# A segment mean over 10 million sorted ids: probe groups spread between data tiles as small row groups, and the masked sums' index ramp kept in PSUM

## The chip, the cores and the metric

The kernel runs on one core of one Trainium2 chip. The metric is the device time of one execution, in microseconds (us); lower is better. Times are quoted as medians of the fast runs of one kernel. Executions of one kernel agree within about 1% (230.13 to 231.72 us before), and a single core has a slower state now and then; slow runs are not compared with fast ones. The engines are called as the profile calls them: DVE is VectorE, ACT is ScalarE, POOL is GpSimd, SP is SyncE, PE is TensorE.

## The reference

```python
n, num_segments = 10_000_000, 10000
data        = np.random.randn(n).astype(np.float32)
segment_ids = np.sort(np.random.randint(0, num_segments, n))      # int64, sorted

def reference(data, segment_ids):
    num_segments = int(segment_ids.max()) + 1
    sums, counts = np.zeros(num_segments, np.float32), np.zeros(num_segments, np.float32)
    np.add.at(sums, segment_ids, data)
    np.add.at(counts, segment_ids, 1)
    return sums / np.maximum(counts, 1)
```

The 40 MB of data must be read. Of the 80 MB of ids only samples are read, because the ids are sorted and a segment is about 1,000 elements long.

## The kernel before

Each of the 128 partitions holds 78,125 consecutive elements, cut into 98 rows of 800. At most one segment border is expected in a row (a check sends any other input down a slow general path, which never runs here). For each row the kernel does this:

1. A *probe load* (SP) reads every 160th id, five 8-byte elements to a row, for a group of rows at once.
2. The *first look* (DVE, small instructions) finds from the probes which 160 elements hold the border, and writes the position into `IDX`.
3. A *gather* (POOL, one for each row, 128 positions) fetches the 159 ids there from HBM into a slot of `GT`.
4. The *reduce* (DVE, six rows at a time) sums those ids; from the sum and `QQ` comes the border's exact place `KK`.
5. The *masked sum* (DVE) adds the elements left of the border, `iota < KK`. ACT adds up the whole row.
6. At the end, counts, carries and two tables put together the means.

```python
GROUPS = [6, 8, 12, 12, 12, 12, 12, 12, 12]      # rows of one probe load
RING = 36                                        # rows that GT can hold
...
iota = cpool.tile([P, L], FP32, name="iota")     # SBUF
GT = gpool.tile([P, RING, W], I64, name="GT")
nc.gpsimd.memset(GT.bitcast(I32).rearrange("p a b -> p (a b)"), 0)

def load_probes(g):
    a = 0 if g == 0 else K * bounds[g] + 1
    b = min(K * bounds[g + 1] + 1, NPR)
    nc.sync.dma_start(out=pr_flat[:, a:b], in_=ids_p[:, a * S : (b - 1) * S + 1 : S])

def first_look(g):
    ...                                           # copy, compare, reduce, scale, subtract
    nc.vector.tensor_add(out=pos, in0=ST[:, a:b], in1=wb[:, a:b])
    nc.vector.scalar_tensor_tensor(out=IDX[:, a:b], in0=NB[:, a:b], scalar=BIG, in1=pos, ...)

def gather(g):
    for r in range(bounds[g], bounds[g + 1]):
        nc.gpsimd.indirect_dma_start(out=GT[:, r % RING, :], in_=ids2d[:],
            in_offset=bass.IndirectOffsetOnAxis(ap=IDX[:, r : r + 1], axis=0), ...)

def second_look(a, b):                            # six rows
    nc.vector.tensor_reduce(out=GS[:, a:b], in_=gt32[:, s : s + b - a, 0 : 2 * W : 2], ...)
    kr = fpool.tile([P, b - a], FP32, name="kr")
    nc.vector.tensor_sub(out=kr, in0=QQ[:, a:b], in1=GS[:, a:b])
    nc.vector.tensor_mul(out=KK[:, a:b], in0=kr, in1=BT[:, a:b])

def split(r):                                     # the masked sum
    nc.vector.scalar_tensor_tensor(out=junk_v[:, 0:n], in0=iota[:, 0:n], scalar=KK[:, r : r + 1],
        in1=d, op0=ALU.is_lt, op1=ALU.mult, accum_out=A[:, r : r + 1])
...
load_probes(0); load_data(0); load_probes(1); load_data(1); load_probes(2)     # (shortened)
for r in range(-6, NR):
    while nt < NT and nt <= (r + 24) // 2:
        load_data(nt)                             # one data tile is two rows
        nt += 1
        if pnext < NG:
            load_probes(pnext)                    # so all nine stand before tile 9
            pnext += 1
    ...                                           # first looks 30 rows ahead, gathers 16 rows ahead
    if r >= done_k: second_look(done_k, min(done_k + 6, NR)); ...
    total(r)
    split(r)
    if r == IF_AT - 4: keys(); check()
    if r == IF_AT: counts(0, 60); with tc.If(...): general_path(...)
    ...
```

The order in which DVE gets its instructions is fixed when the program is built, and it is not the order of this source: in the trace the reduces, first looks and the small work of the check are mixed differently. DVE then works strictly in that order, as far as the traces show: in the changed kernel it stands still for 8.1 us before the reduce at 126.14 us, while five masked sums behind it have their data and their border places.

Of the kernel before, what the change touches and what calls it, by code (L numbers as in the profile page):

```python
# [8 lines left out]
FP32 = mybir.dt.float32  # L9
BF16 = mybir.dt.bfloat16  # L10
I32 = mybir.dt.int32
# [5 lines left out]
P = 128  # L17
D = 78125
L = 800
S = 160  # L20
K = L // S
NR = 98
# [2 lines left out]
E = 8  # L25
NX = NR + E
BIG = float(1 << 24)
GROUPS = [6, 8, 12, 12, 12, 12, 12, 12, 12]
RING = 36
N1 = 72  # L30
N2 = 8
# [146 lines left out]
def kernel(  # L178
# [6 lines left out]
    nc = tc.nc  # L185
    N = data.shape[0]
    NSEG = out.shape[0]
    assert N == P * D and NSEG == 10000 and sum(GROUPS) == NR

# [5 lines left out]
    cpool = ctx.enter_context(tc.tile_pool(name="cpool", bufs=1))  # L195
# [3 lines left out]
    ppool = ctx.enter_context(tc.tile_pool(name="ppool", bufs=1, space=bass.MemoryType.PSUM))  # L199
# [9 lines left out]
    snt = cpool.tile([P, 1], I64, name="snt")  # L209
# [3 lines left out]
    bounds = [0]  # L213
    for g in GROUPS:
        bounds.append(bounds[-1] + g)
# [5 lines that stand above are left out]
# [3 lines left out]
    def load_data(t):  # L224
        d = dpool.tile([P, 2 * L], FP32, name="data_t")
        a, b = 2 * t * L, min(2 * (t + 1) * L, D)
        nc.sync.dma_start(out=d[:, 0 : b - a], in_=data_p[:, a:b])
        tiles[t] = d


    i_i = cpool.tile([P, L], I32, name="i_i")
    iota = cpool.tile([P, L], FP32, name="iota")
    nc.gpsimd.iota(i_i, pattern=[[1, L]], base=0, channel_multiplier=0)
    nc.vector.tensor_copy(out=iota, in_=i_i)
    wb_i = cpool.tile([P, NR], I32, name="wb_i")
    wb = cpool.tile([P, NR], FP32, name="wb")
    nc.gpsimd.iota(wb_i, pattern=[[L, NR]], base=-W, channel_multiplier=D)
# [14 lines left out]
        out=plast, in0=pc, scalar1=float(P - 1), scalar2=1.0e6, op0=ALU.is_equal, op1=ALU.mult  # L252
# [25 lines left out]
    T = cpool.tile([P, NR], FP32, name="T")  # L278
    NB = cpool.tile([P, NX], FP32, name="NB")
    GT = gpool.tile([P, RING, W], I64, name="GT")  # L280
    nc.gpsimd.memset(GT.bitcast(I32).rearrange("p a b -> p (a b)"), 0)  # L281
    gt32 = GT.bitcast(I32)
    junk_v = cpool.tile([P, L], BF16, name="junk_v")
    junk_a = cpool.tile([P, L], BF16, name="junk_a")
# [1 line left out]
    def first_look(g):  # L286
        a, b = bounds[g], bounds[g + 1]
        n = b - a
        if b == NR:
            nc.vector.tensor_copy(out=vend, in_=snt32[:, 0:1])  # L290
            nc.vector.tensor_copy(out=pr32[:, NR - 1, 2 * (K - 1) : 2 * K], in_=snt32)
            nc.vector.tensor_copy(out=V[:, NR : NR + 1], in_=snt32[:, 0:1])
            nc.vector.tensor_copy(out=V[:, a:b], in_=pr32[:, a:b, 0])
        else:
            nc.vector.tensor_copy(out=V[:, a : b + 1], in_=pr32[:, a : b + 1, 0])  # L295
        eq = fpool.tile([P, n, K - 1], FP32, name="eq")
        in1b, in0b = bass.broadcast_tensor_aps(pr32[:, a:b, 0:1], pr32[:, a:b, 2 : 2 * K : 2])
        nc.vector.tensor_tensor(out=eq, in0=in0b, in1=in1b, op=ALU.is_equal)  # L298
        jc = fpool.tile([P, n], FP32, name="jc")
        nc.vector.tensor_reduce(out=jc, in_=eq, axis=AX.X, op=ALU.add)  # L300
        nc.vector.tensor_scalar(  # L301
            out=ST[:, a:b], in0=jc, scalar1=float(S), scalar2=float(1 + W), op0=ALU.mult, op1=ALU.add
        )
        if b == NR:
            nc.vector.tensor_scalar(
                out=ST[:, NR - 1 : NR], in0=ST[:, NR - 1 : NR], scalar1=float(LAST), scalar2=None,
                op0=ALU.min,
            )
        nc.vector.tensor_sub(out=BT[:, a:b], in0=V[:, a + 1 : b + 1], in1=V[:, a:b])  # L309
        nc.vector.tensor_scalar(  # L310
            out=NB[:, a:b], in0=BT[:, a:b], scalar1=-1.0, scalar2=1.0, op0=ALU.mult, op1=ALU.add
        )
        pos = fpool.tile([P, n], FP32, name="pos")
        nc.vector.tensor_add(out=pos, in0=ST[:, a:b], in1=wb[:, a:b])  # L314
        nc.vector.scalar_tensor_tensor(  # L315
            out=IDX[:, a:b], in0=NB[:, a:b], scalar=BIG, in1=pos, op0=ALU.mult, op1=ALU.add
        )
        nc.vector.scalar_tensor_tensor(  # L318
            out=QQ[:, a:b], in0=V[:, a:b], scalar=float(W), in1=ST[:, a:b], op0=ALU.mult, op1=ALU.add
        )  # L320

    def gather(g):
        for r in range(bounds[g], bounds[g + 1]):
            nc.gpsimd.indirect_dma_start(  # L324
                out=GT[:, r % RING, :],
                out_offset=None,
                in_=ids2d[:],
                in_offset=bass.IndirectOffsetOnAxis(ap=IDX[:, r : r + 1], axis=0),
                bounds_check=N - W,
                oob_is_err=False,  # L330
            )

    def second_look(a, b):
        s = a % RING
        nc.vector.tensor_reduce(  # L335
            out=GS[:, a:b], in_=gt32[:, s : s + b - a, 0 : 2 * W : 2], axis=AX.X, op=ALU.add
# [4 lines that stand above are left out]
# [139 lines left out]
    def counts(a, b):  # L480

        n = b - a
        ps = fpool.tile([P, n], FP32, name="ps")
        bp = fpool.tile([P, n], FP32, name="bp")
        ct = fpool.tile([P, n], FP32, name="ct")
        nc.vector.tensor_add(out=ps, in0=rp[:, a:b], in1=KK[:, a:b])
        nc.vector.tensor_mul(out=bp, in0=ps, in1=BT[:, a:b])
        nc.vector.tensor_tensor_scan(
            out=PS[:, a + 1 : b + 1], data0=NB[:, a:b], data1=bp, initial=PS[:, a : a + 1],
            op0=ALU.mult, op1=ALU.add,  # L490
        )
        nc.vector.tensor_sub(out=ct, in0=ps, in1=PS[:, a:b])
        nc.vector.tensor_scalar(out=ct, in0=ct, scalar1=1.0, scalar2=None, op0=ALU.max)
        nc.vector.reciprocal(out=ct, in_=ct)
        nc.vector.scalar_tensor_tensor(
            out=RB[:, PAD + a : PAD + b], in0=ct, scalar=nflag[:, 0:1], in1=BT[:, a:b],
            op0=ALU.mult, op1=ALU.mult,
        )

    def sums(a, b):  # L500

        c = min(b, NR)
        if c > a:
            nc.vector.tensor_sub(out=B[:, a:c], in0=T[:, a:c], in1=A[:, a:c])
# [50 lines left out]
    def write(o, i):  # L555
# [7 lines left out]

    NG = len(GROUPS)
    NT = (NR + 1) // 2
    load_probes(0)
    nc.vector.memset(snt32[:, 0:1], NSEG)
    nc.vector.memset(snt32[:, 1:2], 0)
    nc.sync.dma_start(
        out=snt[0 : P - 1, :],  # L570
        in_=segment_ids[D : N].rearrange("(p d) -> p d", d=D)[:, 0:1],
    )
    load_data(0)
    load_probes(1)
    load_data(1)
    load_probes(2)
    nt = 2

    IF_AT = 64
    C1 = 66  # L580
    C2 = 95
    done_k = 0
    gnext = 0
    lnext = 0
    pnext = 3
    for r in range(-6, NR):
        while nt < NT and nt <= (r + 24) // 2:
            load_data(nt)
            nt += 1
            if pnext < NG:  # L590
                load_probes(pnext)
                pnext += 1
        while lnext < NG and bounds[lnext] <= r + 30:
            first_look(lnext)
            lnext += 1
        while gnext < NG and bounds[gnext] <= r + 16:
            gather(gnext)
            gnext += 1
        if r < 0:
            continue  # L600
        if r >= done_k:
            b = min(done_k + 6, NR)
            second_look(done_k, b)
            done_k = b
        total(r)
        split(r)
        if r == E - 1:
            sums(0, E)
            carry(0, E)
            extend()  # L610
        if r == IF_AT - 4:
            keys()
            check()
        if r == IF_AT:
            counts(0, 60)
            with tc.If(nc.values_load(badi[0:1, 0:1], min_val=0, max_val=1) > 0):
                general_path(
                    tc, fpool, ppool, data, segment_ids, ids2d, odram, rdram, kdram, ident[:, 0:P], fbt
                )
        if r == C1 - 1:  # L620
            counts(60, C1)
            sums(E, C1)
            carry(E, C1)
            select1(0, 12)
            table1(0, 12)
        if done_k == NR and r == 96:
            counts(C1, NX)
            select1(12, N1 // 4)
            select2()
            sums(C1, C2)  # L630
            carry(C1, C2)
            table1(12, N1 // 4)
            write(out1, 0)
# [34 lines left out]
```

## Time and profile before

| | before |
|---|---|
| time, median of 4 fast runs | 231.38 us (230.13 to 231.72) |
| span of the profiled run | 230.0 us |
| DVE busy | 150.9 us (66%) |
| POOL busy | 128.9 us (56%), of it gathers 115.0 |
| first masked sum on DVE | 62.3 us |
| DVE waits for probe loads / for gathers | 40.5 us / 21.5 us |
| last instruction of DVE that counts as busy ends | 217.4 us |

These are the slices of the kernel before: the span in 40 equal parts of 5.75 us, each digit the busy share in tenths. The GB/s line has one number for each slice.

```profile
DVE  4963102204298960351999999999299999999800
POOL 8914777777778777777878788788400000000110
DMA  6899999999999999999999999999749000000000
GB/s 81 102 142 144 231 160 204 239 131 230 237 124 375 409 397 397 398 403 402 399 400 402 399 403 401 401 399 412 303 170 369 14 0 0 0 0 0 2 5 0
```

Until slice 12 (69 us) the DMA engines are busy and move only 81 to 240 GB/s, while the probe loads read single elements of 8 bytes (65,274 of the 74,701 packets of the run are under 512 bytes). Then they move 400 GB/s until the data ends (from 75 to 170 us 1,531 of 7,909 packets are under 512 bytes). DVE is nearly idle at first and full from slice 19 on. From its first gather at 19.7 us POOL is busy in one unbroken row until 164 us.

The costliest groups of the same profile: line, engine, operation, output and inputs, count; then busy time in us and the mean in ns; then the idle time of the engine just before and what ended most of it (`issue`: the engine waited for nothing that the profile shows).

```profile
L324 POOL DMA_INDIRECT GT<-in_segment_ids_dram,IDX x98 | 115.0, 1174 | 36.8 <-issue 26.2
L350 DVE SCALAR_TENSOR_TENSOR junk_v<-iota,q_114,data_t 128x800 bf16<-128x800 f32 x98 | 101.8, 1038 | 0.6
L295 DVE CAST q_114<-pr 128x13 f32<-128x13 int32 (+2 forms) x8 | 9.0, 1127 | 40.5 <-DMA pr<-in_segment_ids_dram 40.5
L335 DVE TENSOR_REDUCE GS<-GT 128x6 f32<-128x954 int32 (+1 forms) x17 | 18.7, 1099 | 23.1 <-DMA GT<-in_segment_ids_dram,IDX 21.5
L281 POOL MEMSET GT<- 128x11448 int32 x1 | 9.6, 9628 | 0.0
```

A gather takes 1.17 us on average and 0.3 us pass between two; apart from those 0.3 us, POOL waits only 10.6 us in all (36.8 - 26.2), most of it before the first gather. DVE's idle time stands in two places: 40.5 us at probe loads and 21.5 us at reduces that wait for gathered ids.

Five single instructions of the timeline (start, duration, instruction, idle time before it):

```profile
2.79 9.63 POOL L281 MEMSET GT<- 128x11448 int32 x1
4.83 7.62 DVE L295 CAST q_114<-pr 128x7 f32<-128x7 int32 x1 [2.39 <-DMA pr<-in_segment_ids_dram]
4.91 7.54 DVE L298 TENSOR_TENSOR eq<-pr 128x24 f32<-128x24 int32 x1
19.69 1.20 POOL L324 DMA_INDIRECT GT<-in_segment_ids_dram,IDX  x1 [7.27 <-DVE IDX L315]
62.31 1.04 DVE L350 SCALAR_TENSOR_TENSOR junk_v<-iota,q_114,data_t 128x800 bf16<-128x800 f32 x1
```

A cast of seven elements takes 7.62 us: it ends with the POOL memset, at 12.4 us. The first masked sum comes at 62.3 us, although its gathers had landed before 40 us.

### The profile page before, as it was taken

How to read it: one execution, taken by the hardware profiler on the slowest of the kernel's cores; microseconds unless marked ns; L12 is line 12 of the kernel's file. 1: busy time of each engine (PE TensorE's matmuls, PEld its weight loads, DVE VectorE, ACT ScalarE, POOL GpSimd, SP SyncE). 2: the span in 40 equal slices, each digit the busy share in tenths (PEclk: the TensorE clock that was granted, in tenths of full speed). 3: DMA queues.
4: the chain of work that ended last, by engine and by line, in shares of the span. 5: the costliest groups of instructions: out<-in, count | busy, mean ns of one | idle time of the engine just before them, and what ended most of it. 6: DMA issues, size and time to landing. Idle time of an engine off the chain costs nothing. (4 is left out here: it accounts for less than half of the span.)

```text
span 230.0 us, 1186 instructions
## 1 busy us (share of the span) xinstructions
PE 1.6 (1%) x6; PEld 1.4 (1%) x6; DVE 150.9 (66%) x432; ACT 95.4 (41%) x197; POOL 128.9 (56%) x114
## 2 busy tenths in 40 slices
PE   0000000000000100000000010000000000000000
PEld 0000000000000100000000000000000000000000
DVE  4963102204298960351999999999299999999800
ACT  2333023033032767676777787667746600000000
POOL 8914777777778777777878788788400000000110
DMA  6899999999999999999999999999749000000000
GB/s 81 102 142 144 231 160 204 239 131 230 237 124 375 409 397 397 398 403 402 399 400 402 399 403 401 401 399 412 303 170 369 14 0 0 0 0 0 2 5 0
DMA packets 74701, 53.39 MB, mean 232 GB/s; under 512 B 65274, under 2 KB 65357, under 8 KB 74688
## 3 DMA queue, kind: packets, MB, share of 16 engines
q1 hardware_dynamic: 69920, 40.51, 62.1%
q0 software_dynamic: 4768, 12.78, 19.2%
q14 instruction: 13, 0.11, 0.2%
HBM read 56.46 MB, written 0.04 MB: 246 GB/s over the span
## 5 line engine op out<-in xcount | busy, mean ns | idle before, releaser
L324 POOL DMA_INDIRECT GT<-in_segment_ids_dram,IDX x98 | 115.0, 1174 | 36.8 <-issue 26.2
L345 ACT ACTIVATE junk_a<-data_t 128x800 bf16<-128x800 f32 x98 | 85.0, 867 | 85.7 <-DMA data_t<-in_data_dram 81.7
L350 DVE SCALAR_TENSOR_TENSOR junk_v<-iota,q_114,data_t 128x800 bf16<-128x800 f32 x98 | 101.8, 1038 | 0.6
L295 DVE CAST q_114<-pr 128x13 f32<-128x13 int32 (+2 forms) x8 | 9.0, 1127 | 40.5 <-DMA pr<-in_segment_ids_dram 40.5
L335 DVE TENSOR_REDUCE GS<-GT 128x6 f32<-128x954 int32 (+1 forms) x17 | 18.7, 1099 | 23.1 <-DMA GT<-in_segment_ids_dram,IDX 21.5
L556 POOL DMA_INDIRECT out_dram<-out_139,AN x1 | 1.1, 1117 | 52.5 <-DVE FF L511 52.5
L345 ACT ACTIVATION_READ_ACCUMULATOR junk_a<-data_t 128x1 f32 x98 | 18.3, 186 | 0.0
L281 POOL MEMSET GT<- 128x11448 int32 x1 | 9.6, 9628 | 0.0
L298 DVE TENSOR_TENSOR eq<-pr 128x48 f32<-128x48 int32 (+2 forms) x9 | 9.2, 1025 | 0.0
L350 DVE DVE_READ_ACCUMULATOR junk_v<-iota,q_114,data_t 128x1 f32 x98 | 7.9, 81 | 0.0
L340 DVE TENSOR_TENSOR q_114<-kr,q_114 128x6 f32<-128x6 f32 (+1 forms) x17 | 2.7, 161 | 0.0
L339 DVE TENSOR_TENSOR kr<-QQ,GS 128x6 f32<-128x6 f32 (+1 forms) x17 | 2.7, 157 | 0.0
L301 DVE TENSOR_SCALAR ST<-jc 128x12 f32<-128x12 f32 (+2 forms) x9 | 2.1, 239 | 0.0
L556 POOL DMA_INDIRECT out_dram<-out_140,AN x1 | 1.0, 992 | 2.0 <-issue 2.0
L310 DVE TENSOR_SCALAR NB<-q_114 128x12 f32<-128x12 f32 (+2 forms) x9 | 1.8, 200 | 0.0
L300 DVE TENSOR_REDUCE jc<-eq 128x12 f32<-128x48 f32 (+2 forms) x9 | 1.7, 194 | 0.0
L345 ACT ACT_TABLE_LOAD x1 | 1.3, 1283 | 0.8 <-PEq L652 0.8
L314 DVE TENSOR_TENSOR pos<-ST,wb 128x12 f32<-128x12 f32 (+2 forms) x9 | 1.5, 164 | 0.1
L309 DVE TENSOR_TENSOR q_114<-q_114 128x12 f32<-128x12 f32 (+2 forms) x9 | 1.5, 166 | 0.1
L318 DVE SCALAR_TENSOR_TENSOR QQ<-q_114,ST 128x12 f32<-128x12 f32 (+2 forms) x9 | 1.5, 164 | 0.1
L315 DVE SCALAR_TENSOR_TENSOR IDX<-NB,pos 128x12 int32<-128x12 f32 (+2 forms) x9 | 1.5, 164 | 0.0
L527 DVE TENSOR_REDUCE out_139<-sel_133 128x48 f32<-128x624 f32 (+1 forms) x2 | 1.3, 628 | 0.0
(95 smaller groups left out, 29.5 us busy)
## 6 DMA issues: line engine op xcount, KB each, us to landing
data_t<-in_data_dram SPq DMA_DIRECT2D x48, 800.0 KB, 11.7
GT<-in_segment_ids_dram,IDX POOLq DMA_INDIRECT x98, 6.1
data_t<-in_data_dram SPq DMA_DIRECT2D x1, 662.5 KB
pr<-in_segment_ids_dram SPq DMA_DIRECT2D x6, 60.0 KB, 11.2
pr<-in_segment_ids_dram SPq DMA_DIRECT2D x1, 58.0 KB, 11.0
pr<-in_segment_ids_dram SPq DMA_DIRECT2D x1, 40.0 KB
pr<-in_segment_ids_dram SPq DMA_DIRECT2D x1, 31.0 KB, 4.0
snt<-in_segment_ids_dram SPq DMA_DIRECT2D x1, 1.0 KB
```

What stands on the lines that cost most here:

```text
L281: nc.gpsimd.memset(GT.bitcast(I32).rearrange("p a b -> p (a b)"), 0)
L295: nc.vector.tensor_copy(out=V[:, a : b + 1], in_=pr32[:, a : b + 1, 0])
L298: nc.vector.tensor_tensor(out=eq, in0=in0b, in1=in1b, op=ALU.is_equal)
L301: nc.vector.tensor_scalar(out=ST[:, a:b], in0=jc, scalar1=float(S), scalar2=float(1 + W), op0=ALU.mult, op1=ALU.add)
L310: nc.vector.tensor_scalar(out=NB[:, a:b], in0=BT[:, a:b], scalar1=-1.0, scalar2=1.0, op0=ALU.mult, op1=ALU.add)
L324: nc.gpsimd.indirect_dma_start(out=GT[:, r % RING, :], out_offset=None, in_=ids2d[:], in_offset=bass.IndirectOffsetOnAxis(ap=IDX[:, r : r ...
L335: nc.vector.tensor_reduce(out=GS[:, a:b], in_=gt32[:, s : s + b - a, 0 : 2 * W : 2], axis=AX.X, op=ALU.add)
L339: nc.vector.tensor_sub(out=kr, in0=QQ[:, a:b], in1=GS[:, a:b])
L340: nc.vector.tensor_mul(out=KK[:, a:b], in0=kr, in1=BT[:, a:b])
L345: nc.scalar.activation(out=junk_a[:, 0:n], in_=d, func=ACT.Copy, accum_out=T[:, r : r + 1])
L350: nc.vector.scalar_tensor_tensor(out=junk_v[:, 0:n], in0=iota[:, 0:n], scalar=KK[:, r : r + 1], in1=d, op0=ALU.is_lt, op1=ALU.mult, accum_ ...
L556: nc.gpsimd.indirect_dma_start(out=out2d[:], out_offset=bass.IndirectOffsetOnAxis(ap=AN[:, i : i + 1], axis=0), in_=o[:], in_offset=None,)
```

## The change

The change has five parts.

1. Eleven smaller probe groups, of 4, 6, 8 and then 10 rows, instead of nine of up to 12.
2. A probe load stands just before the data tile of its first row, instead of all of them before tile 9, so that the data comes in from the start.
3. The first look and its gathers stand 18 rows ahead of the masked sum (30 and 16 before).
4. `iota` lies in PSUM. The masked sum then reads one of its two large operands from PSUM. In the kernel before, the gathers from 21 to 62 us took 1.00 us each, and from the first masked sum on up to 1.83 us; that they would stay at 1.00 us with the ramp out of SBUF was the estimate from these figures.
5. The memset of `GT` is gone, and the check and the branch come at rows 78 and 82 instead of 60 and 64.

```diff
-GROUPS = [6, 8, 12, 12, 12, 12, 12, 12, 12]
+GROUPS = [4, 6, 8, 10, 10, 10, 10, 10, 10, 10, 10]
+X_PROBE = 26
+X_LOOK = 18
...
-    iota = cpool.tile([P, L], FP32, name="iota")
+    iota = ppool.tile([P, 1024], FP32, name="iota")
...
-    nc.gpsimd.memset(GT.bitcast(I32).rearrange("p a b -> p (a b)"), 0)
...
-    for r in range(-6, NR):
-        while nt < NT and nt <= (r + 24) // 2:
+    for r in range(-X_PROBE, NR):
+        while pnext < NG and bounds[pnext] <= r + X_PROBE:
+            load_probes(pnext)
+            pnext += 1
+            ...
+        while nt < NT and 2 * nt <= r + X_PROBE:
             load_data(nt)
             nt += 1
-            if pnext < NG:
-                load_probes(pnext)
-                pnext += 1
-        while lnext < NG and bounds[lnext] <= r + 30:
+        while lnext < NG and bounds[lnext] <= r + X_LOOK:
             first_look(lnext)
+            gather(lnext)
             lnext += 1
-        while gnext < NG and bounds[gnext] <= r + 16:
-            gather(gnext)
-            gnext += 1
...
-        if r == IF_AT - 4:
+        if r == CHECK_AT:                  # 78; IF_AT goes from 64 to 82
             keys()
             check()
...                                         # counts(0, 60), counts(60, C1) become counts(0, C1) after the branch
```

More of the change, by code (lines that the diff above doesn't have):

```diff
@@ L231 @@
     i_i = cpool.tile([P, L], I32, name="i_i")
-    iota = cpool.tile([P, L], FP32, name="iota")
+    iota = ppool.tile([P, 1024], FP32, name="iota")
     nc.gpsimd.iota(i_i, pattern=[[1, L]], base=0, channel_multiplier=0)
-    nc.vector.tensor_copy(out=iota, in_=i_i)
+    nc.vector.tensor_copy(out=iota[:, 0:L], in_=i_i)
     wb_i = cpool.tile([P, NR], I32, name="wb_i")
@@ L565 @@
     NT = (NR + 1) // 2
-    load_probes(0)
     nc.vector.memset(snt32[:, 0:1], NSEG)
     nc.vector.memset(snt32[:, 1:2], 0)
-    nc.sync.dma_start(
-        out=snt[0 : P - 1, :],
-        in_=segment_ids[D : N].rearrange("(p d) -> p d", d=D)[:, 0:1],
-    )
-    load_data(0)
-    load_probes(1)
-    load_data(1)
-    load_probes(2)
-    nt = 2
-    IF_AT = 64
+    CHECK_AT = 78
+    IF_AT = 82
     C1 = 66
@@ L584 @@
     lnext = 0
-    pnext = 3
-    for r in range(-6, NR):
-        while nt < NT and nt <= (r + 24) // 2:
+    pnext = 0
+    nt = 0
+    for r in range(-X_PROBE, NR):
+        while pnext < NG and bounds[pnext] <= r + X_PROBE:
+            load_probes(pnext)
+            pnext += 1
+            if pnext == 2:
+                nc.sync.dma_start(
+                    out=snt[0 : P - 1, :],
+                    in_=segment_ids[D : N].rearrange("(p d) -> p d", d=D)[:, 0:1],
+                )
+        while nt < NT and 2 * nt <= r + X_PROBE:
             load_data(nt)
             nt += 1
-            if pnext < NG:
-                load_probes(pnext)
-                pnext += 1
-        while lnext < NG and bounds[lnext] <= r + 30:
+        while lnext < NG and bounds[lnext] <= r + X_LOOK:
             first_look(lnext)
+            gather(lnext)
             lnext += 1
-        while gnext < NG and bounds[gnext] <= r + 16:
-            gather(gnext)
-            gnext += 1
         if r < 0:
@@ L610 @@
             extend()
-        if r == IF_AT - 4:
+        if r == CHECK_AT:
+            assert lnext == NG
             keys()
@@ L614 @@
         if r == IF_AT:
-            counts(0, 60)
+            assert nt == NT
             with tc.If(nc.values_load(badi[0:1, 0:1], min_val=0, max_val=1) > 0):
@@ L619 @@
                 )
-        if r == C1 - 1:
-            counts(60, C1)
+            counts(0, C1)
             sums(E, C1)
```

## The prediction

> **What bounds the kernel now.** Two phases.
>
> To 70 us the DMA engines do. The slices show them 90% busy, moving only 81 to 240 GB/s: probe loads read single 8-byte elements. In the timeline a 12-row probe load plus a data tile lands every 7.0 us before gathers start, every 9 us beside them; a data tile alone takes 2.0 to 2.6 us. I read: probe load 4.8 us, data tile 2.03, gathered row 0.31, additive. All nine probe loads stand before tile 9, and VectorE (DVE) takes first looks in order, so each waits for its load (40.5 us in the waits view). The first masked sum (L350) starts at 62.3 us.
>
> From 62 us DVE does: 98 masked sums 1.10 us apart, 17 reduces of gathered ids of 1.1 us. It also stands 23 us between 81 and 110 us, at reduces that wait for gathers. Data has ended by 182 us, DVE is full until 217.4: a backlog of 35 us. The span ends 12.6 us later.
>
> **What changes.**
> - Removed: the 9.63 us GpSimd memset of GT. Two DVE instructions take 7.6 us beside it. The first gather comes at 19.7 us, now about 7. Little alone: probes bound this phase.
> - Moved: 11 probe loads between data tiles. DMA work stays: 49 x 2.03 + 98 x 0.31 + 39 for probes + 2 start = 171 us (estimate). Masked sums start near 20 to 25 us.
> - iota in PSUM: a gather takes 1.00 us beside an idle DVE, up to 1.83 beside L350 (mean 1.17, plus 0.3 issue). [...] I now expect all near 1.00. L350 stays about 1.04 us: small DVE instructions that read PSUM here take 0.15 us like others. Little on the end.
> - The check, the branch and the first table go from row 64 to row 82.
>
> **New critical path.** DVE work, about 140 us, fits below DMA. But the last probe load stands before tile 44: it lands at 2 + 39 + 44 x 2.03 + 88 x 0.31 = 157 us. Its first look is placed 18 rows ahead of the split; DVE is held at row 70 to 76 until then, and still has 22 to 28 masked sums (24 to 31 us), reduces (6), check, counts and tables (13), tail (2): 45 to 52 us. DVE ends near 204 us, the span near 217, the time near 218. Of 40 us earlier start only some 13 reach the end; the rest becomes waits for probes in the middle.
>
> **Prediction: 218 us, range 206 to 231.** Faster by over 2%: 0.75; within 2%: 0.19; slower by over 2%: 0.06.
>
> **Signs.** First L350 before 30 us; nine or ten DVE waits on probe loads, 2 to 10 us each, spread to 157 us; data ended near 172; gathers at 1.0 us; DVE not idle in its last 40 us, ending near 204.
>
> **What would make it wrong.** DVE's order is not the source's (base1 of row 60 runs at 19 us), so the last look may sit earlier (near 230) or later (near 207). Probe loads between tiles may not cost 4.8 us. L350 may slow from PSUM: [...]

(Two passages are cut out of this text, since no trace or run of this case shows them: a general reason for the long gathers, and the size of a possible slowing of the masked sum by PSUM. Neither was a term of the forecast's sums, which came to 171, 157, 204, 217 and 218 us and stand complete. What stays for the gathers is the measured 1.00 to 1.83 us; what PSUM did to the masked sum is measured below.)

## The result, and the profile after

A ratio below is the mean time of one kernel's fast runs over the mean of the other's fast runs of the same rounds, with a 95% interval; so it is not quite the ratio of the medians quoted beside it.

| | before | after |
|---|---|---|
| time, median of 4 fast runs | 231.38 us | 240.63 us (240.42 to 240.67) |
| ratio | 1 | 1.041 (1.037 to 1.044) |
| span of the profiled run | 230.0 us | 238.8 us |
| DVE busy | 150.9 us | 143.7 us |
| POOL busy | 128.9 us | 102.4 us |
| first masked sum | 62.3 us | 28.1 us |
| DVE waits for probes / for gathers | 40.5 / 21.5 us | 7.6 / 71.5 us |
| last gather starts | 163.3 us | 203.7 us |

The change made the kernel 4% slower, where 6% faster had been predicted. Both engines have less work, and DVE's masked sums start 34 us earlier. All of that is lost, and 9 us more. The sum on DVE can be closed: busy time fell by 7.2 us; its idle time rose by 16.0 us (from 230.0 - 150.9 = 79.1 to 238.8 - 143.7 = 95.1), of which the waits for gathers are +50.0 and those for probes -32.9. So the question is why DVE waits for gathers.

The slices of the changed kernel (5.97 us each):

```profile
DVE  3140581970992389075708914890993998999800
POOL 3067337277037505730770375057357367200110
DMA  6999999999999999999999999999213223100000
GB/s 144 222 353 256 397 156 402 392 152 395 382 170 405 306 197 417 234 281 411 173 360 401 155 401 397 168 339 362 70 50 105 66 66 96 54 0 0 0 8 0
```

The DMA line is as hoped: data and probes are spread, and the data ends near 168 us. But POOL is no longer one unbroken row. It goes 7 7 0 3 7 5 0 5 7 3 0, and DVE's row has holes at the same rhythm. After 168 us the DMA engines do little, and the last gathers still come until 204 us.

The same groups as shown of before:

```profile
L325 POOL DMA_INDIRECT GT<-in_segment_ids_dram,IDX x98 | 98.2, 1002 | 103.7 <-issue 25.6
L351 DVE SCALAR_TENSOR_TENSOR junk_v<-iota,q_114,data_t 128x800 bf16<-128x800 f32 x98 | 102.0, 1040 | 0.6
L336 DVE TENSOR_REDUCE GS<-GT 128x6 f32<-128x954 int32 (+1 forms) x17 | 18.8, 1107 | 71.8 <-DMA GT<-in_segment_ids_dram,IDX 71.5
L296 DVE CAST q_114<-pr 128x11 f32<-128x11 int32 (+3 forms) x10 | 1.7, 169 | 7.6 <-DMA pr<-in_segment_ids_dram 7.6
```

A gather now takes 1.00 us, and the masked sum takes no longer with the ramp in PSUM (1,040 against 1,038 ns; from start to start, with nothing between two, 1.09 against 1.10 us). But POOL stands idle 103.7 us before its gathers, and only 25.6 us of that are the gaps of 0.3 us. The waits view says what ended the rest (engine, waiting line, releaser; us in total, times, longest):

```profile
DVE GS L336 <- DMA GT<-in_segment_ids_dram,IDX: 71.5, 12, 12.0
...
POOL GT L325 <- DVE IDX L316: 24.9, 3, 9.5
...
POOL GT L325 <- DVE q_114 L341: 19.5, 2, 10.0
POOL GT L325 <- DVE kr L340: 13.5, 2, 8.6
POOL GT L325 <- DVE pos L315: 10.5, 1, 10.5
DVE q_114 L296 <- DMA pr<-in_segment_ids_dram: 7.6, 2, 6.0
```

DVE waits for POOL, and POOL waits for DVE. (The releasers L341, L340 and L315 stand next to the index computation L316 in DVE's queue, as the timeline below shows for one of them; I read all four as waits for `IDX`. The 10.5 us of L315 are the wait before the very first gather, at 13.3 us, and no turn.) One turn of this, in the timeline:

```profile
91.13 0.17 DVE L316 SCALAR_TENSOR_TENSOR IDX<-NB,pos 128x10 int32<-128x10 f32 x1
91.57 0.99 POOL L325 DMA_INDIRECT GT<-in_segment_ids_dram,IDX  x1 [9.53 <-DVE q_114 L341]
...
101.35 1.15 DVE L336 TENSOR_REDUCE GS<-GT 128x6 f32<-128x954 int32 x1 [5.60 <-DMA GT<-in_segment_ids_dram,IDX]
...
103.29 0.99 POOL L325 DMA_INDIRECT GT<-in_segment_ids_dram,IDX  x1 [0.30 <-issue]
...
110.27 1.15 DVE L336 TENSOR_REDUCE GS<-GT 128x6 f32<-128x954 int32 x1 [4.12 <-DMA GT<-in_segment_ids_dram,IDX]
...
112.45 0.16 DVE L316 SCALAR_TENSOR_TENSOR IDX<-NB,pos 128x10 int32<-128x10 f32 x1
...
112.89 1.00 POOL L325 DMA_INDIRECT GT<-in_segment_ids_dram,IDX  x1 [8.60 <-DVE kr L340]
```

Read it so. At 91.13 us DVE writes the positions of rows 38 to 47. POOL gathers them from 91.57 to 104.28 us, one every 1.30 us. Each lands about 6 us after its issue (the median of all gathers is 5.8 us, 6.1 in the kernel before). The reduce at 110.27 us is that of rows 42 to 47, so it needs the very last of these ten gathers, and DVE stands at it for 4.1 us. The positions of the next ten rows, 48 to 57, stand *behind* this reduce in DVE's queue. So they are written at 112.45 us, and POOL has stood idle for 8.6 us. Then it begins again: the index computations of the fifth to the tenth group stand at 68.9, 91.1, 112.5, 133.9, 156.7 and 174.3 us, 21.1 us apart on average, although ten gathers need only 13. (The eleventh follows at 191.4 us, 17.1 us later: the data loads had ended, and its predecessors' gathers landed after 2.9 us instead of about 6.)

The probes were not late: the probe load of rows 48 to 57 was issued at 70.5 us and landed at most 17.2 us later, 25 us before its index computation. It lay ready and DVE came to it too late.

I call the *lead* of a group the number of rows between the rows already reduced and the group's first row, at the point where its index computation stands in DVE's queue. It is counted from the order of the instructions. The lead is what POOL may have under way while DVE waits for a reduce:

| kernel | lead of each group from the fifth on, in rows |
|---|---|
| before (groups of 12) | 38, 50, 62, 62, 26 |
| after (groups of 10) | 4, 2, 0, 4, 2, 0, 4 |

At a lead of 0 to 4 rows DVE and POOL take turns here.

### The profile page after: what moved, and what is told of

Read it like the earlier page. It is cut to its first block, busy times and chain, and to the rows that moved or that the text cites. A ratio compares the mean times of both kernels' runs of the same rounds, so it can differ in the third digit from the quotient of the medians.

```text
span 238.8 us, 1190 instructions
## 1 busy us (share of the span) xinstructions
PE 1.6 (1%) x6; PEld 1.4 (1%) x6; DVE 143.7 (60%) x443; ACT 95.4 (40%) x197; POOL 102.4 (43%) x113
## 5 line engine op out<-in xcount | busy, mean ns | idle before, releaser
L325 POOL DMA_INDIRECT GT<-in_segment_ids_dram,IDX x98 | 98.2, 1002 | 103.7 <-issue 25.6
L351 DVE SCALAR_TENSOR_TENSOR junk_v<-iota,q_114,data_t 128x800 bf16<-128x800 f32 x98 | 102.0, 1040 | 0.6
L336 DVE TENSOR_REDUCE GS<-GT 128x6 f32<-128x954 int32 (+1 forms) x17 | 18.8, 1107 | 71.8 <-DMA GT<-in_segment_ids_dram,IDX 71.5
L296 DVE CAST q_114<-pr 128x11 f32<-128x11 int32 (+3 forms) x10 | 1.7, 169 | 7.6 <-DMA pr<-in_segment_ids_dram 7.6
L341 DVE TENSOR_TENSOR q_114<-kr,q_114 128x6 f32<-128x6 f32 (+1 forms) x17 | 2.7, 159 | 0.1
L340 DVE TENSOR_TENSOR kr<-QQ,GS 128x6 f32<-128x6 f32 (+1 forms) x17 | 2.7, 160 | 0.1
L299 DVE TENSOR_TENSOR eq<-pr 128x40 f32<-128x40 int32 (+3 forms) x11 | 2.1, 187 | 0.0
L301 DVE TENSOR_REDUCE jc<-eq 128x10 f32<-128x40 f32 (+3 forms) x11 | 2.0, 184 | 0.0
L310 DVE TENSOR_TENSOR q_114<-q_114 128x10 f32<-128x10 f32 (+3 forms) x11 | 1.8, 166 | 0.0
L302 DVE TENSOR_SCALAR ST<-jc 128x10 f32<-128x10 f32 (+3 forms) x11 | 1.8, 166 | 0.0
L319 DVE SCALAR_TENSOR_TENSOR QQ<-q_114,ST 128x10 f32<-128x10 f32 (+3 forms) x11 | 1.8, 162 | 0.0
L311 DVE TENSOR_SCALAR NB<-q_114 128x10 f32<-128x10 f32 (+3 forms) x11 | 1.8, 163 | 0.0
L316 DVE SCALAR_TENSOR_TENSOR IDX<-NB,pos 128x10 int32<-128x10 f32 (+3 forms) x11 | 1.8, 161 | 0.0
L315 DVE TENSOR_TENSOR pos<-ST,wb 128x10 f32<-128x10 f32 (+3 forms) x11 | 1.8, 160 | 0.0
```

The lines of the kernel that those rows point to most:

```text
L299: nc.vector.tensor_tensor(out=eq, in0=in0b, in1=in1b, op=ALU.is_equal)
L301: nc.vector.tensor_reduce(out=jc, in_=eq, axis=AX.X, op=ALU.add)
L302: nc.vector.tensor_scalar(out=ST[:, a:b], in0=jc, scalar1=float(S), scalar2=float(1 + W), op0=ALU.mult, op1=ALU.add)
L310: nc.vector.tensor_sub(out=BT[:, a:b], in0=V[:, a + 1 : b + 1], in1=V[:, a:b])
L311: nc.vector.tensor_scalar(out=NB[:, a:b], in0=BT[:, a:b], scalar1=-1.0, scalar2=1.0, op0=ALU.mult, op1=ALU.add)
L325: nc.gpsimd.indirect_dma_start(out=GT[:, r % RING, :], out_offset=None, in_=ids2d[:], in_offset=bass.IndirectOffsetOnAxis(ap=IDX[:, r : r ...
```

## The experiments

The theory, called A below and in the texts on record: the loss comes from this lead, so from the order on DVE's queue; the spread of the probe loads shrinks it, and the other parts of the change are harmless or useful. The rivals: that another part of the change costs the time (the smaller groups, the ramp in PSUM, the later branch), or that not the lead but the place of the probe loads in the DMA queue itself does. What was expected stands in each place as it was written before the run. One caution: these texts do not count the lead in rows, as above, but the masked sums between an index computation and the reduce that needs its gathers; and the text of e7 went by whichever reduce came next, and failed.

A build, without a run, came first: making `X_LOOK` 22 or 26 instead of 18, so that the source asks for the first look earlier, compiles to the identical program on every engine. In the changed kernel the lead cannot be set by that constant; it follows other things, above all the place of the probe loads among the data loads.

Runs e1 to e4 were made on one chip in one session in which the kernel before was slow in six of seven executions; its one fast run was 232.26 us, so its fast time there was the same as elsewhere within 0.4%. No ratio is given for them; their medians are set beside the 240.63 us of the changed kernel. (That their own runs agree does not prove them fast. For e1 there is a check: its near twin e8, made in a good session, took 222.50 us.) Runs e5 to e15 have ratios to the kernel before, at 231.4 to 232.0 us.

### e1: the changed kernel with the reduces held in place

The reduce writes into the scratch tile of the masked sum. The two then depend on each other through that tile, and the build must leave them in the source's order.

```diff
-    junk_v = cpool.tile([P, L], BF16, name="junk_v")
+    junk_v = cpool.tile([P, L], FP32, name="junk_v")
...
-            out=GS[:, a:b], in_=gt32[...], axis=AX.X, op=ALU.add
+            out=junk_v[:, 0 : b - a], in_=gt32[...], axis=AX.X, op=ALU.add
...
-        nc.vector.tensor_sub(out=kr, in0=QQ[:, a:b], in1=GS[:, a:b])
+        nc.vector.tensor_sub(out=kr, in0=QQ[:, a:b], in1=junk_v[:, 0 : b - a])
```

> The kernel after the change, but each reduce of gathered ids writes into the scratch tile that the masked sums also write, so the compiled order must keep it directly in front of the masked sums of its own six rows (source order). Theory A (the compiled VectorE order puts a reduce some 3 to 5 masked sums behind the index computation its gathers need, so VectorE and the gathers take turns): the 71.5 us of waits for gathers fall to 15 to 35 us and the time to 190 to 210 us. Rival B (probe loads between data tiles hold VectorE or the data back): waits move to the probe loads, time 230 to 242 us. Rival C (late check, branch and last look set the end): time stays above 230 us.

Measured: 220.86 us (220.65 to 221.50), 20 us less than the changed kernel, but 11 us above the range of A and below those of the rivals. The leads became 4, 8, 6, 10, 8, 12, 10. The waits moved from gathers to probes (12.0 of the 21.1 us for gathers lie before the very first reduce, as in the changed kernel):

```profile
DVE junk_v L336 <- DMA GT<-in_segment_ids_dram,IDX: 21.1, 4, 12.0
DVE q L296 <- DMA pr<-in_segment_ids_dram: 17.8, 4, 6.3
DVE q L296 <- issue: 9.9, 2, 6.1
DVE q L294 <- DMA pr<-in_segment_ids_dram: 4.5, 1, 4.5
```

This is the picture that the prediction had drawn: the last first look (L294) starts at 161.1 us (predicted: its load lands at 157), DVE's last reduce ends at 206.7 (predicted 204), and the time is 220.9 (predicted 218). So the prediction's sums come out nearly right when DVE's order is close to the one it assumed: 72 masked sums stand before the last index computation, where it had said row 70 to 76. The new order, with the scratch that enforces it, is worth 20 us here; e5 looks at what that edit itself does.

### e2: the changed kernel, probe loads 14 rows ahead of their data

```diff
-X_PROBE = 26
-X_LOOK = 18
+X_PROBE = 40
+X_DATA = 26
+X_LOOK = 26
...
-        while nt < NT and 2 * nt <= r + X_PROBE:
+        while nt < NT and 2 * nt <= r + X_DATA:
```

> The kernel after the change, but each probe load is issued 14 rows (7 data tiles) further ahead of the data. Theory A: the reduces stay some 3 masked sums behind their index computation, because both are moved up together, so the waits for gathers remain 50 to 70 us and the time is 215 to 235 us. Rival B (probes come too late): time falls to 190 to 210 us, with waits for gathers below 35 us.

Measured: 238.35 us (237.71 to 239.98), above the range expected. DVE still waited 53.4 us for gathers. The compiled order shows why: the reduces had moved forward together with the index computations. The leads are 10, 2, 6, 4, 2, 6, 4. (DVE also stands 9.8 us, and ACT 10.0 us, at stops for which the profile shows no releaser, as in e3 below.) The edit missed its aim, and that is itself a result: probes that come earlier do not help as long as the lead stays short.

### e3: both edits together

> Both edits of the two runs before. Theory A: the index computation is now some 15 masked sums in front of its reduce, the waits for gathers fall to 5 to 25 us, time 185 to 205 us, the data transfers bound it. Rival B: no better than the run with early probes alone.

The edits are those of e1 and e2. Measured: 224.72 us (224.04 to 229.17, the last slow), clearly above the range expected. The waits for gathers fell to 11.9 us and the leads are 16 to 22, as the theory wanted. In their place DVE stands some 25 us in all and ACT 14 us, most of it between 47 and 75 us of the span, at stops for which the profile shows no releaser ("issue" or "remote"). What these stops are I could not settle. So a long lead takes the waits for gathers away, but the 20 us more that were hoped for did not come.

### e4: the changed kernel with the ramp back in SBUF

```diff
-    iota = ppool.tile([P, 1024], FP32, name="iota")
+    iota = cpool.tile([P, L], FP32, name="iota")
```

> The kernel after the change, but the index ramp is back in SBUF. Theory A: gathers again take up to 1.8 us beside a masked sum (mean 1.1 instead of 1.00), each group of ten takes 1 to 2 us longer, and since VectorE waits for gathers this costs 3 to 12 us: 242 to 252 us. Rival D (PSUM operand is what slowed the kernel): 228 to 234 us.

Measured: 253.80 us (253.17 to 254.43), 1.8 us above the range of A. The two lines of its profile:

```profile
L325 POOL DMA_INDIRECT GT<-in_segment_ids_dram,IDX x98 | 110.0, 1123 | 103.5 <-DVE IDX L316 29.3
L336 DVE TENSOR_REDUCE GS<-GT 128x6 f32<-128x954 int32 (+1 forms) x17 | 18.8, 1107 | 84.7 <-DMA GT<-in_segment_ids_dram,IDX 83.8
```

The gathers take 1.12 us again instead of 1.00, and 12 us more of them stand in the chain of turns. So PSUM is not what made the change slow: it saves about 13 us of it. (Two of the last reduces also stand elsewhere in this build, so the 13 us are not all the gathers'.)

### e5: the kernel before with the reduces held in place

The edit is that of e1.

> The kernel before, with only the reduces kept in source order by the same edit as in the first run. Theory A (a reduce that stands early in the compiled order makes VectorE wait for gathers): the waits for gathers between 81 and 110 us and at 162 us (27 us) mostly go, the first masked sum stays near 62 us because of the probes, time 210 to 223 us. If the edit helps the changed kernel for another reason (for instance the fp32 scratch), it gains under 3 us here: 228 to 233 us.

Measured: 230.07 us, ratio 0.994 (0.989 to 0.998): 7 us above the range of A, and in the range of the rival (228 to 233), that the edit helps e1 for another reason. The waits for gathers are gone, as A expected. But DVE's busy time rose from 150.9 to 157.9 us: held in place, a reduce, its subtraction and its multiplication mostly stand one behind the other with nothing between them. The three then take 1.58 us to the start of the next masked sum (1.18, 0.20 and 0.20); in the kernel before, with independent work behind each, the next instruction starts after 1.06, 0.08 and 0.08 us. A masked sum takes 1,048 ns, against 1,038. The gain was spent on that, on 6.0 us of waiting for the last probe load (0.8 before), and on a stop of 5.3 us behind the branch. Two things follow. In the kernel before, taking away the 21.5 us of waits for gathers gains some 1.5 us, since other work and stops take their place. And the edit itself makes nothing faster on DVE: in e1 too its busy time rose, by 4.8 us, and a masked sum took 1,045 ns against 1,040. This speaks against the rival, and the 20 us of e1 are probably an underestimate of what the order costs.

### e6: the kernel before with the ramp in PSUM

```diff
-    iota = cpool.tile([P, L], FP32, name="iota")
+    iota = ppool.tile([P, 1024], FP32, name="iota")
```

> The kernel before, with only the index ramp moved to PSUM. Theory A: gathers all take about 1.00 us, so the 98 end 10 to 16 us earlier than 164 us, the waits for gathers shrink from 27 us to 10 to 20 us, time 218 to 228 us. Rival: gathers are off the path in this kernel, time 229 to 233 us.

Measured: 224.24 us, ratio 0.969 (0.964 to 0.973), as expected. One edit, and the gathers are down from 1.17 to 1.00 us:

```profile
L324 POOL DMA_INDIRECT GT<-in_segment_ids_dram,IDX x98 | 97.9, 999 | 37.1 <-issue 27.8
```

The waits for gathers fell from 21.5 to 14.9 us. This part of the change is a gain by itself. (The build also moved the lead of the eighth group from 62 to 56 rows.)

### e7: the kernel before without the memset

```diff
-    nc.gpsimd.memset(GT.bitcast(I32).rearrange("p a b -> p (a b)"), 0)
```

> The kernel before, with only the GpSimd memset of the gather ring taken out. First gather about 8 us earlier. The compiled order changes with it: the index computations of groups 5 to 9 now stand between masked sums, directly in front of a reduce, as in the changed kernel. Theory A: the first masked sum comes before 50 us, yet waits for gathers rise to 40 to 70 us, time 228 to 245 us. Rival (the memset is a plain cost at the start): 221 to 226 us.

Measured: 215.19 us, ratio 0.929 (0.925 to 0.933); the profiled run itself was slow, at 218.22 us. Both theories had expected more time (228 to 245 and 221 to 226 us). A's text had read the build as putting the index computations directly in front of a reduce, as in the changed kernel, and expected turns; counted against their own reduces, they lead by 26 rows. Removing 9.6 us on an engine that is not the limit took 16 us off the time. The build without the memset has another order on DVE: the fifth to ninth group now have a lead of 26 rows each (38, 50, 62, 62, 26 before), so the first reduces and masked sums no longer stand behind the first looks of seven groups. The first masked sum:

```profile
36.59 1.05 DVE L349 SCALAR_TENSOR_TENSOR junk_v<-iota,q,data_t 128x800 bf16<-128x800 f32 x1
```

It comes at 36.6 us instead of 62.3, with the same loads in the same order on SP; the first gather did not move (19.6 us, 19.7 before). So "probe loads bound the kernel until 70 us" was not the whole reading: what held the masked sums was that DVE's queue put seven first looks, each waiting for its probe load, ahead of them (and the beginning of an eighth, which waited 6.4 us). Too long a lead costs at the start what too short a lead costs later.

### e8: e1 with the probe loads 8 rows ahead

```diff
-X_PROBE = 26
+X_PROBE = 40
+X_DATA = 32
...
-        while nt < NT and 2 * nt <= r + X_PROBE:
+        while nt < NT and 2 * nt <= r + X_DATA:
```

> The changed kernel with the reduces in source order and each probe load 8 rows (4 data tiles) further ahead of the data. Theory A: with gathers out of the way VectorE of the first run was held by the probe loads (some 32 us of waits there, last look at 161 us); they come 8 to 10 us earlier here, waits for probes 10 to 22 us, time 208 to 217 us. Rival: the rest of the time is set by something else, 219 to 226 us.

Measured: 222.50 us, ratio 0.961 (0.956 to 0.965), in the range of the rival. The leads are 10 to 18, the waits for gathers 12.2 us, but those for probes 38.4 us. With the reduces held, a longer lead no longer helped.

### e9: the kernel before with the ramp in PSUM and without the memset

The edits are those of e6 and e7.

> The kernel before with two parts of the change: ramp in PSUM, memset gone; the probe loads, group sizes, looks, gathers and the check stay as before. Theory A (the spreading of the probe loads does the harm, by breaking the gather stream; these two parts help): gathers run nearly without a break at 1.3 us, time 204 to 213 us. Rival (the gain of the memset's removal already holds the gain of PSUM): 213 to 217 us.

Measured: 217.64 us, ratio 0.941 (0.939 to 0.943): above both ranges, and no better than e7 alone. The gathers take 1.00 us (1.19 in e7), and the leads are the same 26. But DVE stands 11.1 us at the copy of `fbt` behind the branch, until 169.8 us, and the profile gives SP, at the branch, as what ended the stop. In the source the general path may write `fbt`, a small table. That SP comes to the branch so late because of the data loads that stand before it is my reading, not shown by itself; it fits e5, where the same stop ends at 169.6 us and SP's next two data loads follow at 170.3. The two gains do not add up: beside e7's profile, which is of a slow run, the waits for gathers fell by 8.2 us (37.0 to 28.8), and the stop grew by as much (2.9 to 11.1).

### e10: the changed kernel with the probe loads early, all else kept

Only SP's loads change their order: one probe load goes ahead of each of the first eleven data tiles, as in the kernel before. Small groups, ramp in PSUM, no memset, late branch stay.

```diff
-        while pnext < NG and bounds[pnext] <= r + X_PROBE:
-            load_probes(pnext)
-            pnext += 1
-            ...
         while nt < NT and 2 * nt <= r + X_PROBE:
+            if pnext < NG:
+                load_probes(pnext)
+                pnext += 1
+            ...
             load_data(nt)
             nt += 1
```

> The changed kernel with all of its parts (groups of 4, 6, 8 and 10, look joined with gather, check at row 78, branch at 82, PSUM, no memset), but one probe load in front of each of the first eleven data tiles, as in the kernel before. Theory A: each index computation now stands about ten masked sums in front of the reduce that needs its gathers; waits for gathers 20 to 40 us instead of 71.5; GpSimd's idle time in front of gathers under 60 us instead of 103.7; time 203 to 217 us. Rival C (late check, branch, joined look and gather, small groups do the harm): 228 us or more.

Measured: 215.18 us, ratio 0.931 (0.929 to 0.933), inside the range of A; the rival is out. The leads are now 16, 14, 18, 16, 14, 18, 16. The slices of DVE and POOL (5.33 us each), and DVE's waits:

```profile
DVE  4330272443999329899989985999999307999600
POOL 4017777777777777777777777760000000000110
```

```profile
DVE GS L336 <- DMA GT<-in_segment_ids_dram,IDX: 21.7, 5, 5.4
DVE q L296 <- DMA pr<-in_segment_ids_dram: 14.0, 4, 5.1
...
DVE junk_v L351 <- DMA data_t<-in_data_dram: 11.1, 8, 4.6
DVE sel L521 <- SPq L613: 10.0, 1, 10.0
```

```profile
L325 POOL DMA_INDIRECT GT<-in_segment_ids_dram,IDX x98 | 98.3, 1003 | 42.0 <-issue 28.9
```

POOL's row is unbroken again, and the last gather starts at 142.1 us (203.7 in the changed kernel). POOL's idle time before gathers fell, with the same buffers, from 103.7 to 42.0 us, of which 28.9 are the gaps of 0.3 us and 12.5 the wait before the first gather. The waits for gathers fell from 71.5 to 21.7 us. This is the run that isolates the part of the change that does the harm: of the five parts of the change, undoing the second alone turns +4.1% into -6.9%.

### e11: the changed kernel with the old groups

```diff
-GROUPS = [4, 6, 8, 10, 10, 10, 10, 10, 10, 10, 10]
+GROUPS = [6, 8, 12, 12, 12, 12, 12, 12, 12]
```

> The changed kernel with the group sizes of before (6, 8, seven of 12), probe loads still spread between data tiles. Theory A: the turn-taking stays, with fewer and longer turns: waits for gathers 55 to 80 us, time 228 to 246 us. Rival (small groups do the harm): under 220 us.

Measured: 242.76 us, ratio 1.050 (1.045 to 1.056), as A expected. Every group from the third on has a lead of 2 rows; DVE waits 70.1 us for gathers. So the size of the groups is not the cause.

### e12: e10 with the old groups

Both edits, of e10 and of e11.

> The changed kernel with early probe loads and the old group sizes: all that stays of the change is PSUM, no memset, look joined with gather, late check and branch. Theory A: as the run with early loads and small groups, or a little faster since the gathers lead by more: 202 to 215 us. Rival C: 228 us or more.

Measured: 219.82 us, ratio 0.950 (0.948 to 0.952), 5 us above the range of A, far from the rival. The waits for gathers are 41.0 us, at leads of 14 for groups of 12 (14 to 18 for groups of 10 in e10). Beside e10 it shows that the smaller groups, taken alone, are worth 4.6 us once the probes are early.

### e13: the changed kernel, probe loads 24 rows ahead

```diff
-X_PROBE = 26
-X_LOOK = 18
+X_PROBE = 44
+X_DATA = 20
+X_LOOK = 26
...
-        while nt < NT and 2 * nt <= r + X_PROBE:
+        while nt < NT and 2 * nt <= r + X_DATA:
```

(The text on record calls this one edit. As the diff shows, the data's own constant is moved by 6 rows too, and `X_LOOK`, as in e2. That `X_LOOK` does nothing was shown for the changed kernel only. In builds without a run, setting it back to 18 changes one lead here, the sixth group's from 20 to 14, and one in e2, from 2 to 8.)

> The changed kernel with one edit: the probe load of a group is issued 24 rows before its data instead of together with it (they stay spread between the data tiles to the end). Compiled order of VectorE: indices of groups 5, 6 and 7 now stand 13, 11 and 10 masked sums ahead of the reduce that needs them, as in e10; those of the last groups still only 2 to 4 ahead (3 to 5 for all in the changed kernel). Theory A (too few masked sums between an index computation and its own reduce make VectorE and GpSimd take turns): gathers run as one stream to about row 57, then turns of about 22 us return for the last three or four groups; 217 to 231 us, VectorE's wait for gathers 35 to 60 us. Rival (what counts is that the probe loads are out of the queue early, as in e10 and before): probes still run to the end, so 235 us or more.

Measured: 218.78 us (217.53 to 220.28), ratio 0.946 (0.940 to 0.952), inside the range of A. This is the dose between the changed kernel and e10: the leads are 28, 20, 18, then 10, 8, 6, 4. The index computations of the groups with a lead of 10, 8, 6 and 4 stand at 95.5, 109.1, 127.1 and 147.3 us. So the turn grows from 13.6 to 18.0 and 20.2 us as the lead shrinks, where 13.0 us is the unhindered pace of ten gathers and 21.1 the mean of the changed kernel.

```profile
DVE GS L337 <- DMA GT<-in_segment_ids_dram,IDX: 41.4, 9, 6.6
```

The waits for gathers, 41.4 us, lie between the 71.5 and the 21.7. The probe loads still run spread between the data tiles, the last at 120.6 us. In e2 it was issued at 125.5 us, nearly the same place, at leads of 2 to 6 rows from the sixth group on, and e2 took 238.35 us. So the rival, that the place of the probes itself counts and not the lead, is out.

### e14 and e15: what holds e10

In e10 DVE stands for 10.0 us at the copy of `fbt`. In e14 the first table (selection and sum) goes from the branch to row 96; in e15 the check and branch go to rows 84 and 92.

```diff
 e14
         if done_k == NR and r == 96:
+            select1(0, 12)
+            table1(0, 12)
             counts(C1, NX)                       # both calls taken out at r == IF_AT
 e15
-    CHECK_AT = 78
-    IF_AT = 82
+    CHECK_AT = 84
+    IF_AT = 92
```

> e10 (probes early, all else of the change kept) with the first table's selection and sum moved from the branch to row 96. In e10 VectorE stood 10.0 us at the copy of fbt, which the branch can write, waiting for SyncE to reach the branch. Theory: the wait goes away, since the copy now stands behind the last reduces; 204 to 211 us. Rival: VectorE then waits at the branch or for late data instead, 212 us or more.

> e10 with the check at row 84 and the branch and first table at row 92 (row 78 and 82 in e10). SyncE's last data loads are then issued before VectorE comes to the branch, and the last reduces stand before it (two of three by the compiled order). Theory: the 10.0 us wait at the fbt copy shrinks; 205 to 212 us. Rival (the end is bound by data or by VectorE's own work): 213 us or more.

Measured: e14 211.00 us, ratio 0.911 (0.908 to 0.914), at the upper edge of the range; e15 212.31 us, ratio 0.918 (0.914 to 0.921), 0.3 us above the range and below the rival's. The stop shrank from 10.0 to 6.0 us in e14 and 2.0 in e15. It did not vanish in e14, since the build moved the copy forward again, to just behind the branch:

```profile
DVE sel L521 <- SPq L613: 6.0, 1, 6.0
```

DVE leaves that copy at 177.3 us in e10 and 177.8 and 177.5 us in e14 and e15: SP comes to the branch at the same time in all three, 17 us after it issued its last data load. What was won is that more work stands before it. e14 is the fastest kernel, 8.9% below the kernel before, and both it and e10 beat both kernels.

### The leads and times together

| kernel | lead from the fifth group on | DVE's waits for gathers | POOL idle before gathers | time, us |
|---|---|---|---|---|
| e4 (ramp in SBUF) | 4, 2, 0, 4, 2, 0, 4 | 83.8 | 103.5 | 253.8 |
| e11 | 2, 2, 2, 2, 2 | 70.1 | 104.8 | 242.8 |
| after | 4, 2, 0, 4, 2, 0, 4 | 71.5 | 103.7 | 240.6 |
| e2 | 10, 2, 6, 4, 2, 6, 4 | 53.4 | 90.3 | 238.4 |
| before | 38, 50, 62, 62, 26 | 21.5 | 36.8 | 231.4 |
| e6 | 38, 50, 62, 56, 26 | 14.9 | 37.1 | 224.2 |
| e12 | 20, 14, 14, 14, 14 | 41.0 | 45.6 | 219.8 |
| e13 | 28, 20, 18, 10, 8, 6, 4 | 41.4 | 59.6 | 218.8 |
| e9 | 26, 26, 26, 26, 26 | 28.8 | 46.3 | 217.6 |
| e10 | 16, 14, 18, 16, 14, 18, 16 | 21.7 | 42.0 | 215.2 |
| e7 (profile of a slow run) | 26, 26, 26, 26, 26 | 37.0 | 46.3 | 215.2 |
| e15 | 16, 14, 18, 16, 14, 18, 16 | 26.6 | 42.3 | 212.3 |
| e14 | 16, 14, 18, 16, 14, 18, 16 | 21.3 | 42.6 | 211.0 |

(The kernels whose reduces are held in place are left out, since that edit has its own cost.) At 6 rows and less the engines take turns. POOL's idle time shows it best: the gaps of 0.3 us make some 29 us of it and the wait before the first gather 7 to 17, so at leads of 14 and more hardly anything else is left. The 21 to 41 us for which DVE still waits there I read as the mere pace of gathering, 1.30 us a row. At 38 and more, masked sums wait for first looks of far later rows. The best times stand between. Lead and probe placement are not free of each other in this kernel, so the table is an ordering and not a law. Note e7: the kernel before, without its memset and with nothing else changed, is as fast as e10.

## Why the prediction was wrong

It said 218 us and 0.75 for faster; measured are 240.6 us, slower by 4.1% and outside the range.

- **What bounds the kernel before.** Partly right. The DMA engines do work slowly until 69 us, and each probe load delays the first looks. But e7 starts its masked sums at 36.6 us with the same loads. The step from "the DMA engines are busy with probes" to "the masked sums can't start earlier" left out DVE's queue.
- **The memset.** Right that it goes and that the seven-element cast beside it falls from 7.62 to 0.17 us. "Little alone: probes bound this phase" was wrong: alone it is worth 16 us (e7), and since the first gather did not move, through the order that the build then chooses. "The first gather comes at 19.7 us, now about 7" was wrong too: it came at 13.3 us, since the first index computation stood in DVE's queue behind the first look of the second group, which waited 6.0 us for its probe load.
- **Masked sums start near 20 to 25 us.** Nearly right: 28.1 us.
- **The ramp in PSUM: gathers all near 1.00 us, masked sums unchanged.** Right: 1,002 ns and 1,040 ns. Moving the ramp alone took the mean gather from 1,174 to 999 ns (e6), and moving it back brought 1,123 (e4); what in the hardware does this no run shows. "Little on the end" was wrong: it is worth 7 us before (e6) and about 13 us in the changed kernel (e4).
- **Data ended near 172 us, the last probe load at 157.** Right: 168 us, and the last probe load was issued at 137.9 and landed at most 17.2 us later, by 155.1.
- **"Its first look is placed 18 rows ahead of the split; DVE is held at row 70 to 76 until then".** This is the step that failed. It took the place in DVE's queue from the source. In the compiled order first looks stand only 0 to 4 rows ahead of the rows already *reduced*. DVE was then not held by probe loads ("nine or ten DVE waits on probe loads": two, 7.6 us) but by gathers (twelve, 71.5 us). The last first look came at 186.5 us, 31 us after its probes had landed, and DVE ended at 226.1 instead of 204 us. The prediction did name the risk: "DVE's order is not the source's". But it allowed for one look being a little off, up to 230 us, not for every look being tied to a reduce.
- **The picture itself was nearly sound.** With the reduces held in the source's order (e1), the numbers of the prediction come true within about 4 us: 161, 206.7 and 220.9 against 157, 204 and 218. Some luck is in this: e1 also waits 21.1 us for gathers, and the first looks stand 9 to 16 masked sums ahead and not 18.

So the mechanism of the loss is a new wait, not a lost gain: the spread made the build place each group's index computation behind a reduce that needs nearly the last gather of the group before, so DVE and POOL, which had worked side by side, took turns. Why the build chooses this place is only inferred: moving nothing but loads moved it (e10 beside the changed kernel, e8 beside e1), so it seems to follow from when the build expects the probes to be there. No run shows its reasons.

Two things stay open. The stops of e2 and e3 without a shown releaser; and e8, where a longer lead with held reduces gave waits for probes and no gain.

## What to carry to other kernels

Where an engine works through its instructions in a fixed order, as DVE did in these traces, a producer's small instruction should stand ahead of the consumer's wait by at least the time that the other engine needs, here one group of ten gathers at 1.30 us and a landing of 6 us, which a lead of 14 to 18 rows gave in e10. Here less (0 to 6 rows) made the two engines take turns, and much more (38 to 62 rows) held early work behind late loads. When loads are moved, look at where the build then places the small instructions in the in-order queue before counting any gain: count them in the compiled order, since the source and the busy shares don't show it. And let loads that only feed such small instructions come early even if they are inefficient: here that cost a slow start and won 25 us against spreading them (e10). Loads that stay spread but come 24 rows sooner won 22 (e13).
